# A paired first modulation, a later second modulation and a 32-byte tile in an encoder layer

## The chip, the cores and the metric

The kernel runs on one core of a Trainium2 chip. A core has five engines with queues of their own: TensorE (PE) multiplies matrices, VectorE (DVE) and ScalarE (ACT) work elementwise, GpSimd (POOL) too, and SyncE (SP) mostly issues DMA transfers. They run side by side and wait for each other through semaphores. The metric is the device time of one execution in microseconds (us), the median over runs.

## The reference

One bidirectional encoder layer in float32, 512 tokens of 2048 features. A condition vector c gives six modulation vectors of 2048 each; these are summed over all rows of a 2048 x 12288 matrix, which is 100.7 MB to read.

```
mod = silu(c) @ w_ada + b_ada
sh1, sc1, gt1, sh2, sc2, gt2 = split(mod, 6)
h    = rms_norm(x, g_norm1) * (1 + sc1) + sh1
proj = h @ w_in                        # 8 differential heads, latent q and kv
mix  = concat(diff_attention, latent_attention) @ w_out
x    = x + gt1 * mix
h2   = rms_norm(x, g_norm2) * (1 + sc2) + sh2
x    = x + gt2 * ((silu(h2 @ w_gate) * (h2 @ w_up)) @ w_down)
```

## The kernel before, in words

**Products.** Each float32 operand is split into a rounded high half and the rest (`hi`, `lo`), and a product is three matmuls: hi*hi, hi*lo, lo*hi (`mm3`, lines 241 to 243, in that order on PE). For a weight, `Weights` (lines 60 to 100) loads `raw` by SP (lines 73 and 77, three buffers), ScalarE rounds it to `hi` (line 89), and VectorE or GpSimd subtracts for `lo` (line 97). Which of the two does it stands in the plan of the weights, as "dve", "pool" or "alt" (by turns).

**Modulation sums.** A modulation vector is a sum over the 2048 rows of `w_ada`. A row tile is loaded by SP (line 301), and VectorE multiplies it by a column of silu(c) and adds it to an accumulator `adaacc` (line 305 for the first, line 308 for the rest: scalar_tensor_tensor). A last sum over partitions is a small matmul against ones (`ps_ada`, line 327), and lines 328 to 330 make the columns G and SH from it.

**First stage, to about 180 us.** The 16 blocks of 128 features are taken in the pieces `BLOCKS` = (0,2), (2,2), (4,4), (8,4), (12,4) (start, count). For each piece scale and shift are summed in two accumulators, the normalised x is transposed and modulated (line 378, `hT` split in lines 380 to 382), and the input projection of five heads goes on with that piece (`ps_in`). Partial sums are kept in `raw_in` (line 488). The loads of the modulation use five `araw` buffers; so SP's next load waits for an addition.

**Heads, to about 780 us.** The other heads, the attention, and the first half of the second modulation run interleaved.

**Output projection, about 780 to 930 us.** Four blocks `b` of 512 columns (`ps_o`). Beside them runs a generator `mod2` (line numbers around 1040) that loads and sums the second half of the second modulation, in two groups of four blocks: per group 32 steps that load and sum, six that do nothing, and one that makes the columns. It is taken forward `MOD_PACE[b]` steps per step of the projection. After each block VectorE does the residuals (lines 1053 and 1054, on GpSimd for some), SP stores them to `x1d` (line 1100), ScalarE squares and sums them (line 1102). In the last block a reduction (line 1104) and a reciprocal root on GpSimd (lines 260 and 261) follow each of the four row tiles. Then come the transposes (`ps_xT`, line 1060) and the broadcast of the root (`ps_r`, line 1111).

**Gate and up, about 930 to 1800 us.** First two 256-column pieces in the direct way (`gate_up`, `ps_g` and `ps_u`). Between its products `second_norm` makes the normalised and modulated h2 (lines 1134 to 1136). Then a Strassen-like scheme with seven products of half size (lines 1235 to 1237).

**Down projection, to the end.** `ps_d`, with the activations (`ax`) as stationary operand and the weights' `hi` and `lo` as moving operand.

**Order.** PE's order is the order in which the code issues it. The other four engines get theirs from a scheduler. Each engine works its own queue in order, SP's included.

Of the kernel before, what the change touches and what calls it, by code (L numbers as in the profile page):

```python
# [18 lines left out]
P = 128  # L19
# [117 lines left out]
def weight_plan(a):  # L137
# [61 lines left out]
def hybrid_layer(ctx, tc, a, out):  # L199
# [120 lines left out]

    def ada_columns(sums, k0, nk, G, SH, cg, cbs, cbh):
# [31 lines left out]
    def accs0(dt=F32):  # L353
        return st[1].tile([P, 512], dt, tag="acc", bufs=4, name="adaacc")
# [9 lines left out]
    def modulation_sums(k0, nk):  # L364
        yield from ada_sums(raws0, accs0, 1, 0, k0, nk, 8 // nk, sums1[k0])
# [706 lines left out]
    for b in range(4):  # L1072
# [87 lines left out]
    def gate_up(j, between):  # L1160
# [4 lines left out]
        for k4 in range(4):  # L1165
            for n, pp in (("gate", pg), ("up", pu)):
# [3 lines left out]
                for i in range(4):  # L1170
# [3 lines left out]
                    if G2_done[0] < 4:  # L1174
                        next(mod2, None)
# [177 lines left out]
    gt2 = fd[1].tile([P, D], F32, name="gt2")  # L1353

# [17 lines left out]
    load_acts(1)  # L1372
    W = Wd
# [53 lines left out]
MOD_PACE = (0.3, 2.8, 3.4, 3.2)  # L1427
# [40 lines left out]
```

## Time and profile before

| | |
|---|---|
| median of three runs | 2329.75 us (2326.13 to 2329.98) |
| the profiled execution, its own time | 2330.51 us |
| span in its trace | 2328.1 us |
| PE busy | 2208.3 us (95%) |
| DVE busy | 1634.0 us (70%) |
| ACT busy | 944.7 us (41%) |
| POOL busy | 442.9 us (19%) |
| DMA | 344.98 MB, mean 148 GB/s |

The span runs from the first to the last recorded instruction; the execution's own time is 2.4 us longer. PE is busy nearly all the time, but not in the first eighth and not around 800 to 1000 us. A busy share is an average over stages, so the table of stretches below takes them apart. A row of the timeline gives start, duration, engine, line and operation with the tiles it writes and reads; a bracket at its end holds the idle time before it and what ended it. Rows of PE overlap, since matmuls are pipelined: their pitch, from start to start, is what counts.

### The profile page before, as it was taken

The numbers are of one execution on the slowest core, as the hardware profiler recorded it, in microseconds if no ns is written. First come the engines' busy times: TensorE is split into PE (matmuls) and PEld (weight loads), VectorE is DVE, ScalarE is ACT, GpSimd is POOL, SyncE is SP. The second block draws the span as 40 slices with busy tenths as digits, with TensorE's granted clock in tenths as the row PEclk, the third lists the DMA queues.
The fourth block names the chain that finished last, engine by engine and source line by source line (L and its number), as shares of the span: only waits on it lengthen the run. The fifth ranks groups of instructions, "written<-read, shape, count | busy, mean of one in ns | idle before, by whom it ended". The sixth has DMA issues, their size and how long they took to land.

```text
span 2328.1 us, 35444 instructions
## 1 busy us (share of the span) xinstructions
PE 2208.3 (95%) x13878; PEld 2011.6 (86%) x13878; DVE 1634.0 (70%) x2365; ACT 944.7 (41%) x1569; POOL 442.9 (19%) x492
## 2 busy tenths in 40 slices
PE   2799999999989997999999999999999999999999
PEld 2799989998877785789999999999999877888887
DVE  6987777868898575847777777777777577232543
ACT  4423545566555222434444444444444522121211
POOL 0002433445553622210000000000000221222221
PEclk9899999999999998999999999999999999999999
DMA  9965345422442585243333333333333775232532
GB/s 298 323 216 147 103 138 156 139 88 85 152 157 79 191 286 182 78 131 118 127 115 121 111 126 119 123 112 121 118 127 118 247 263 195 99 128 91 170 129 99
DMA packets 270569, 344.98 MB, mean 148 GB/s; under 512 B 14749, under 2 KB 170886, under 8 KB 270274
## 3 DMA queue, kind: packets, MB, share of 16 engines
q1 hardware_dynamic: 269912, 342.37, 44.9%
q8 instruction: 108, 1.77, 0.3%
q10 hardware_dynamic: 490, 0.36, 0.1%
q14 instruction: 59, 0.48, 0.1%
HBM read 322.71 MB, written 19.96 MB: 147 GB/s over the span
## 4 chain that ended last, share of the span: by engine, by line
PE 57%; DVE 6%; DMA 4%; issue 1%; ACT 1%; SPq 0%; POOL 0%; DVEq 0%; ACTq 0%
PE ps_d L243 6%; PE ps_d L241 6%; PE ps_d L242 6%; PE ps_X L1235 5%; PE ps_X L1236 5%; PE ps_X L1237 5%; PE ps_W L1235 3%; PE ps_W L1236 3%; PE ps_W L1237 3%; DVE adaacc L308 2%; DMA araw<-in_w_ada_dram 2%; PE ps_Y L1235 2%; PE ps_Z L1235 2%; PE ps_Y L1236 2%; PE ps_Z L1236 2%; PE ps_Z L1237 2%
## 5 line engine op out<-in xcount | busy, mean ns | idle before, releaser
L97 POOL TENSOR_TENSOR lo<-raw,hi 128x1024 fp32r<-128x1024 f32 (+1 forms) x75 | 183.6, 2448 | 1403.3 <-ACT hi L89 1384.5
L89 ACT CAST hi<-raw 128x1024 fp32r<-128x1024 f32 (+2 forms) x228 | 221.0, 970 | 508.4 <-PE ps_d L242 286.6
L97 DVE TENSOR_TENSOR lo<-raw,hi 128x768 fp32r<-128x768 f32 (+2 forms) x153 | 168.5, 1101 | 188.5 <-ACT hi L89 184.2
L1235 PE MATMUL ps_X<-comb,wh 128*128 128x256 f32 x960 | 269.7, 281 | 0.0
L1218 ACT CAST wh<-wr 128x1024 fp32r<-128x1024 f32 x160 | 168.6, 1054 | 247.5 <-PE ps_X L1236 69.1
L1236 PE MATMUL ps_X<-comb,wh 128*128 128x256 f32 x960 | 268.8, 280 | 0.0
L1237 PE MATMUL ps_X<-comb,wl 128*128 128x256 f32 x960 | 266.9, 278 | 0.0
L243 PE MATMUL ps_d<-lo,ax 128*128 128x512 f32 x640 | 254.7, 398 | 6.5 <-DVE lo L97 6.5
L241 PE MATMUL ps_d<-hi,ax 128*128 128x512 f32 x640 | 254.3, 397 | 0.0
L242 PE MATMUL ps_d<-hi,ax 128*128 128x512 f32 x640 | 254.1, 397 | 0.0
L1201 DVE TENSOR_TENSOR wl<-wr,wh 128x1024 fp32r<-128x1024 f32 x160 | 195.6, 1222 | 80.2 <-ACT wh L1218 80.0
L241 PE MATMUL ps_in<-hi,hh 128*128 128x384 f32 (+2 forms) x704 | 236.5, 336 | 6.1 <-ACT hi L89 2.7
L243 PE MATMUL ps_in<-lo,hh 128*128 128x384 f32 (+2 forms) x704 | 230.9, 328 | 8.5 <-DVE lo L97 8.5
L242 PE MATMUL ps_in<-hi,hl 128*128 128x384 f32 (+2 forms) x704 | 230.2, 327 | 0.6 <-DVE hl L382 0.6
L1218 ACT CAST wh<-wt 128x1024 fp32r<-128x1024 f32 x120 | 126.2, 1051 | 197.5 <-PE ps_X L1236 120.9
L1201 DVE TENSOR_TENSOR wl<-wt,wh 128x1024 fp32r<-128x1024 f32 x120 | 146.8, 1223 | 81.1 <-ACT wh L1218 81.1
L1236 PEld LDWEIGHTS ps_X<-comb,wh 128*128 128x128 f32 x960 | 180.5, 188 | 0.0
L1237 PEld LDWEIGHTS ps_X<-comb,wl 128*128 128x128 f32 x960 | 180.5, 188 | 0.0
L1235 PE MATMUL ps_W<-comb,wh 128*128 128x256 f32 x640 | 180.0, 281 | 0.4 <-DVE cu L1246 0.4
L1235 PEld LDWEIGHTS ps_X<-comb,wh 128*128 128x128 f32 x960 | 180.2, 188 | 0.0
L1236 PE MATMUL ps_W<-comb,wh 128*128 128x256 f32 x640 | 179.2, 280 | 0.0
L1237 PE MATMUL ps_W<-comb,wl 128*128 128x256 f32 x640 | 177.9, 278 | 0.0
(319 smaller groups left out, 5533.4 us busy)
## 6 DMA issues: line engine op xcount, KB each, us to landing
araw<-in_w_ada_dram SPq DMA_DIRECT2D x96, 512.0 KB
raw<-in_w_down_dram SPq DMA_DIRECT2D x88, 512.0 KB
wr<-in_w_gate_dram SPq DMA_DIRECT2D x40, 1024.0 KB
wr<-in_w_up_dram SPq DMA_DIRECT2D x40, 1024.0 KB
ada<-in_w_ada_dram SPq DMA_DIRECT2D x128, 256.0 KB
raw<-in_w_in_dram SPq DMA_DIRECT2D x128, 192.0 KB
raw<-in_w_out_dram SPq DMA_DIRECT2D x32, 512.0 KB
x<-in_w_ada_dram SPq DMA_DIRECT2D x64, 256.0 KB
```

The costliest lines, as they stand in the source:

```text
L89: nc.scalar.copy(out=hi[:, :n], in_=raw[:, :n])
L97: e.tensor_tensor(out=lo[:, :n], in0=raw[:, :n], in1=hi[:, :n].bitcast(F32), op=ALU.subtract)
L241: pe.matmul(o, ah, bh, start=start, stop=False)
L242: pe.matmul(o, al, bh, start=False, stop=False)
L243: pe.matmul(o, ah, bl, start=False, stop=stop)
L308: dve.scalar_tensor_tensor(out=acc[:, :width], in0=raw[:, i, :width], scalar=c_col[:, q:q + 1], in1=acc[:, :width], op0=ALU.mult, op1=ALU.add)
L1201: dve.tensor_tensor(out=out, in0=x, in1=y, op=ALU.subtract)
L1218: act.copy(out=hi, in_=src)
L1235: pe.matmul(ps[bk], wh[:, k], c[:, 0], start=first and k == 0, stop=False, skip_group_check=True)
L1236: pe.matmul(ps[bk], wh[:, k], c[:, 1], start=False, stop=False, skip_group_check=True)
L1237: pe.matmul(ps[bk], wl[:, k], c[:, 0], start=False, stop=k == 7, skip_group_check=True)
```

## The change

**First modulation.** A new generator `ada_pair` loads scale and shift columns of a row tile into one `araw` tile, laid out row group, scale or shift, column, and sums both in one operation on one accumulator of up to 1024 columns. Two accumulators of 1024 replace four of 512. The two 256-column pieces load two row groups per tile, one DMA each.

**Second modulation.** `MOD_PACE` falls in the last three blocks. 74.4 steps are taken in the projection instead of 100, of 78 that there are. The rest is taken in `second_norm(12)`; the step that stood in `gate_up`'s inner loop is gone. The stores to `x1d` move from SP's queue to ACT's, after each block's residuals. The four reductions and roots of the last block become one of 128x4.

**Weights.** The direct gate and up pieces get "dve" in place of "alt".

**The tile.** A tile of eight floats per partition is allocated in the pool `fd` of the down stage. It is never used. The tiles of that pool, `ax` among them, come to lie 32 bytes lower in each partition.

```
--- before.py
+++ after.py
@@ -180,7 +180,7 @@
     for j in range(STRAIGHT):
         for k4 in range(4):
             for n in ("gate", "up"):
-                plan.append(((n, j, k4), [4, 256], rows(a["w_" + n][0], k4 * 512, 4, j * 256, 256), "alt"))
+                plan.append(((n, j, k4), [4, 256], rows(a["w_" + n][0], k4 * 512, 4, j * 256, 256), "dve"))
     return plan
 
 
@@ -318,6 +318,26 @@
                     yield None
             sums.append(acc)
 
+    def ada_pair(raws, accs, p_scale, p_shift, k0, nk, sums):
+
+        n = nk * P
+        acc = accs()[:, :2 * n].rearrange("p (s n) -> p s n", s=2)
+        nq = 512 // n
+        both = w_ada[:, :, p_shift * D:(p_scale + 1) * D].rearrange("p q (s n) -> p q s n", s=2)
+        for j in range(KC // nq):
+            raw = raws()[:, :2 * nq * n].rearrange("p (q s n) -> p q s n", q=nq, s=2)
+            for i in range(nq):
+                sp.dma_start(out=raw[:, i], in_=both[:, nq * j + i, :, k0 * P:k0 * P + n])
+            for i in range(nq):
+                q = nq * j + i
+                if q == 0:
+                    dve.tensor_scalar(out=acc, in0=raw[:, i], scalar1=c_col[:, 0:1], scalar2=None, op0=ALU.mult)
+                else:
+                    dve.scalar_tensor_tensor(out=acc, in0=raw[:, i], scalar=c_col[:, q:q + 1], in1=acc, op0=ALU.mult,
+                                             op1=ALU.add)
+            yield None
+        sums += [acc[:, 1], acc[:, 0]]
+
     def ada_columns(sums, k0, nk, G, SH, cg, cbs, cbh):
 
         ks = slice(k0, k0 + nk)
@@ -351,7 +371,7 @@
         return st[1].tile([P, 1024], F32, tag="araw", bufs=5, name="araw")
 
     def accs0(dt=F32):
-        return st[1].tile([P, 512], dt, tag="acc", bufs=4, name="adaacc")
+        return st[1].tile([P, 1024], dt, tag="acc", bufs=2, name="adaacc")
 
     ssq1 = st[1].tile([P, NT, 4], F32, name="ssq1")
     rstd1 = st[1].tile([P, NT], F32, name="rstd1")
@@ -362,7 +382,7 @@
     sums1 = {k0: [] for k0, _ in BLOCKS}
 
     def modulation_sums(k0, nk):
-        yield from ada_sums(raws0, accs0, 1, 0, k0, nk, 8 // nk, sums1[k0])
+        yield from ada_pair(raws0, accs0, 1, 0, k0, nk, sums1[k0])
 
     def modulation(k0, nk):
         for b in range(1, 4):
@@ -1097,12 +1117,12 @@
                 transposes(b - 1, spare[0])
         for t in range(NT):
             residual(pss, b, t, gt1, pool if t in OUT_POOL and b < 3 else dve)
-            sp.dma_start(out=x1d[t * P:(t + 1) * P, b * 512:(b + 1) * 512], in_=x1[t][b])
             sq = tmp("sq")
             act.activation(sq, x1[t][b], AF.Square, accum_out=ssq2[:, t, b:b + 1])
-            if b == 3:
-                dve.tensor_reduce(out=rstd2[:, t:t + 1], in_=ssq2[:, t, :], axis=AX.X, op=ALU.add)
-                rsqrt(rstd2[:, t:t + 1], rstd2[:, t:t + 1], 1.0 / D)
+        for t in range(NT):
+            act.dma_start(out=x1d[t * P:(t + 1) * P, b * 512:(b + 1) * 512], in_=x1[t][b])
+    dve.tensor_reduce(out=rstd2, in_=ssq2, axis=AX.X, op=ALU.add)
+    rsqrt(rstd2, rstd2, 1.0 / D)
     while G2_done[0] < 3:
         next(mod2)
     transposes(3, spare[0])
@@ -1128,7 +1148,7 @@
 
     def second_norm(k0):
         while G2_done[0] <= k0 // 4:
-            next(mod2)
+            next(mod2, None)
         for kc in range(k0, k0 + 4):
             xt = x1T[kc]
             dve.scalar_tensor_tensor(out=xt, in0=xt, scalar=G2[:, kc:kc + 1], in1=rB, op0=ALU.mult, op1=ALU.mult)
@@ -1171,8 +1191,6 @@
                     kc = k4 * 4 + i
                     for m in range(2):
                         mm3(pp[m], wh[:, i, tsl(m)], wl[:, i, tsl(m)], h2(kc, 0), h2(kc, 1), kc == 0, kc == KC - 1)
-                    if G2_done[0] < 4:
-                        next(mod2, None)
                 next(between, None)
         sg = wp.tile([P, 1024], F32, tag="raw", bufs=3, name="sg").rearrange("p (m s) -> p m s", m=2)
         for m in range(2):
@@ -1351,6 +1369,7 @@
     fd = open_pool("fd", "right")
     sums = [[fd[1].tile([P, 512], F32, tag="sums", bufs=16, name="sums") for _ in range(4)] for _ in range(NT)]
     gt2 = fd[1].tile([P, D], F32, name="gt2")
+    pads = []
 
     def gate2():
         def raws():
@@ -1370,6 +1389,7 @@
 
     side = gate2()
     load_acts(1)
+    pads.append(fd[1].tile([P, 8], F32, name="pad"))
     W = Wd
     n_parts = len(PARTS)
     j = 0
@@ -1424,7 +1444,7 @@
 DIFF_SIDE = (1, 2, 1, 2, 1, 2, 1, 1)
 MLA_SIDE = (1, 2)
 MOD_EARLY = 8
-MOD_PACE = (0.3, 2.8, 3.4, 3.2)
+MOD_PACE = (0.3, 2.0, 2.5, 2.5)
 MLA_STEPS = "s0 F t0 e F1 t1 s1 v0 F t2 F1 v1 t3 s2 F v2 F1 o0 v3 F o2 o3 s3 o1 F1"
 MLA_FILL = (16.0, 15.7, 16.0, 0.2, 14.1, 19.0, 3.3, 12.8)
```

VectorE's order in the first stage, before: the end of the second piece (numbers at names tell buffers apart; `lo` are low halves of input weights).

```order
L308 SCALAR_TENSOR_TENSOR adaacc_270<-araw_289,c_col_73,adaacc_270 128x256
L308 SCALAR_TENSOR_TENSOR adaacc_295<-araw_296,c_col_73,adaacc_295 128x256
L308 SCALAR_TENSOR_TENSOR adaacc_270<-araw_289,c_col_73,adaacc_270 128x256
L308 SCALAR_TENSOR_TENSOR adaacc_295<-araw_302,c_col_73,adaacc_295 128x256
L308 SCALAR_TENSOR_TENSOR adaacc_270<-araw_289,c_col_73,adaacc_270 128x256
L308 SCALAR_TENSOR_TENSOR adaacc_295<-araw_302,c_col_73,adaacc_295 128x256 x3
L308 SCALAR_TENSOR_TENSOR adaacc_295<-araw_308,c_col_73,adaacc_295 128x256 x2
L97 TENSOR_TENSOR lo_328<-raw_324,hi_327 128x768
L308 SCALAR_TENSOR_TENSOR adaacc_295<-araw_308,c_col_73,adaacc_295 128x256
L97 TENSOR_TENSOR lo_380<-raw_331,hi_379 128x768
L308 SCALAR_TENSOR_TENSOR adaacc_295<-araw_308,c_col_73,adaacc_295 128x256
L305 TENSOR_SCALAR adaacc_358<-araw_359,c_col_73 128x512
```

And now, at the same place:

```order
L336 SCALAR_TENSOR_TENSOR adaacc_261<-araw_277,c_col_73,adaacc_261 128x512 x2
L336 SCALAR_TENSOR_TENSOR adaacc_261<-araw_282,c_col_73,adaacc_261 128x512 x2
L336 SCALAR_TENSOR_TENSOR adaacc_261<-araw_287,c_col_73,adaacc_261 128x512 x2
L336 SCALAR_TENSOR_TENSOR adaacc_261<-araw_292,c_col_73,adaacc_261 128x512 x2
L336 SCALAR_TENSOR_TENSOR adaacc_261<-araw_297,c_col_73,adaacc_261 128x512 x2
L97 TENSOR_TENSOR lo_310<-raw_306,hi_309 128x768
L97 TENSOR_TENSOR lo_360<-raw_313,hi_359 128x768
L334 TENSOR_SCALAR adaacc_340<-araw_341,c_col_73 128x1024
L336 SCALAR_TENSOR_TENSOR adaacc_340<-araw_344,c_col_73,adaacc_340 128x1024
```

One sum of 512 stands where two of 256 stood, and the sums of the second piece are all ahead of the first two low halves, which stood among them.

PE's order around the second group's columns, before (`ps_o` is the output projection):

```order
L241 MATMUL ps_o<-hi,mh 128x512
L242 MATMUL ps_o<-hi,ml 128x512
L243 MATMUL ps_o<-lo,mh 128x512
L327 MATMUL ps_ada<-ones,adaacc 128x1 x8
L241 MATMUL ps_o<-hi,mh 128x512
L242 MATMUL ps_o<-hi,ml 128x512
L243 MATMUL ps_o<-lo,mh 128x512
```

And now (`ps_g` and `ps_u` are gate and up):

```order
L241 MATMUL ps_u<-comb,hi 128x512
L242 MATMUL ps_u<-comb,lo 128x512
L243 MATMUL ps_u<-comb,hi 128x512
L347 MATMUL ps_ada<-ones,adaacc 128x1 x8
L241 MATMUL ps_g<-comb,hi 128x512
L242 MATMUL ps_g<-comb,lo 128x512
L243 MATMUL ps_g<-comb,hi 128x512
```

The columns left the last block of the output projection for the direct gate and up piece, 96 matmuls behind `ps_r`.

VectorE's order at the end of the output projection, before:

```order
L308 SCALAR_TENSOR_TENSOR adaacc<-x_9708,c_col,adaacc 128x512
L308 SCALAR_TENSOR_TENSOR adaacc<-x_9723,c_col,adaacc 128x512
L328 TENSOR_TENSOR G_95<-ps_ada,small 128x4
L330 TENSOR_TENSOR SH_96<-ps_ada,small 128x4
L329 TENSOR_TENSOR G_95<-G_95,small 128x4
L1157 TENSOR_TENSOR shs<-SH_96 128x8
L97 TENSOR_TENSOR lo<-raw,hi 128x1024
L1053 TENSOR_TENSOR tm<-ps_o,gt_8892 128x512
L1054 TENSOR_TENSOR x_8879<-x_8879,tm 128x512
L1053 TENSOR_TENSOR tm<-ps_o,gt_8892 128x512
L1104 TENSOR_REDUCE rstd_8875<-ssq_8874 128x1
L1054 TENSOR_TENSOR x_8883<-x_8883,tm 128x512
```

And now:

```order
L1073 TENSOR_TENSOR tm<-ps_o,gt_8823 128x512
L308 SCALAR_TENSOR_TENSOR adaacc<-x_9815,c_col,adaacc 128x512
L1074 TENSOR_TENSOR x_8810<-x_8810,tm 128x512
L308 SCALAR_TENSOR_TENSOR adaacc<-x_9818,c_col,adaacc 128x512
L1073 TENSOR_TENSOR tm<-ps_o,gt_8823 128x512
L1074 TENSOR_TENSOR x_8814<-x_8814,tm 128x512
L1073 TENSOR_TENSOR tm<-ps_o,gt_8823 128x512
L97 TENSOR_TENSOR lo<-raw,hi 128x1024
L1074 TENSOR_TENSOR x_8818<-x_8818,tm 128x512
L1073 TENSOR_TENSOR tm<-ps_o,gt_8823 128x512
L1074 TENSOR_TENSOR x_8822<-x_8822,tm 128x512
L1124 TENSOR_REDUCE rstd_8806<-ssq_8805 128x4
```

The last sums stand beside the first residual of the last block instead of ahead of the columns' G and SH, and one reduction of 128x4 follows the last residual.

## Rows read from the trace of the kernel before

**Rows 1.** The table of stretches: per engine busy us (instructions), then granted clock, DMA share, rate.
```profile
41.00:120.00 79.00, 60.73 (x319) 57.20 (x320) 77.56 (x137) 35.34 (x59) 0.00 (x0) 0.91 0.99 322
...
802.00:900.00 98.00, 81.42 (x376) 66.73 (x374) 80.92 (x96) 26.77 (x46) 26.56 (x12) 0.94 0.83 274
...
930.00:1030.00 100.00, 95.60 (x417) 78.00 (x418) 68.56 (x105) 42.69 (x63) 19.11 (x7) 0.97 0.31 99
1030.00:1850.00 820.00, 819.61 (x6826) 813.19 (x6825) 617.65 (x641) 364.47 (x452) 8.20 (x5) 1.00 0.38 126
```

**Rows 2.** What TensorE waited for, 0 to 320 us: total us, times, longest us.
```profile
PE ps_ada L327 <- DVE adaacc L308: 36.1, 4, 17.4
PE ps_in L243 <- DVE lo L97: 8.5, 4, 5.6
```

**Rows 3.** The table of stretches, two windows of ten microseconds.
```profile
50.00:60.00 10.00, 8.10 (x49) 7.67 (x49) 9.96 (x21) 4.18 (x8) 0.00 (x0) 1.00 1.05 354
100.00:110.00 10.00, 4.46 (x24) 3.81 (x23) 10.00 (x18) 4.75 (x8) 0.00 (x0) 0.86 0.90 296
```

**Rows 4.** What the SyncE queue waited for, 0 to 180 us.
```profile
SPq L301 <- DVE adaacc L308: 58.9, 44, 4.0
```

**Rows 5.** Lines by form, VectorE, 0 to 180 us: busy us, mean ns, idle before.
```profile
L308 DVE SCALAR_TENSOR_TENSOR adaacc<-araw,c_col,adaacc 128x512 f32<-128x512 f32 x90 | 66.4, 744 | 0.2
L308 DVE SCALAR_TENSOR_TENSOR adaacc<-araw,c_col,adaacc 128x256 f32<-128x256 f32 x60 | 28.0, 482 | 7.8 <-DMA araw<-in_w_ada_dram 6.6
```

**Rows 6.** TensorE's timeline in the first stage: start us, us, instruction.
```profile
113.18 0.52 PE L241 MATMUL ps_in<-hi,hh 128*128 128x384 f32 x1
...
117.76 0.33 PE L241 MATMUL ps_in<-hi,hh 128*128 128x384 f32 x1
...
119.00 0.33 PE L242 MATMUL ps_in<-hi,hl 128*128 128x384 f32 x1
```

**Rows 7.** TensorE's timeline in the output projection; idle before in brackets.
```profile
899.63 1.87 PE L327 MATMUL ps_ada<-ones,adaacc 128*128 128x1 f32 x8 [10.95 <-DVE adaacc L308]
...
901.93 0.63 PE L242 MATMUL ps_o<-hi,ml 128*128 128x512 f32 x1
...
905.77 0.49 PE L242 MATMUL ps_o<-hi,ml 128*128 128x512 f32 x1
```

**Rows 8.** VectorE's timeline in the output projection.
```profile
880.67 0.75 DVE L308 SCALAR_TENSOR_TENSOR adaacc<-x,c_col,adaacc 128x512 f32<-128x512 f32 x1 [2.65 <-DMA x<-in_w_ada_dram]
881.33 1.22 DVE L97 TENSOR_TENSOR lo<-raw,hi 128x1024 fp32r<-128x1024 f32 x1
...
887.52 2.85 DVE L308 SCALAR_TENSOR_TENSOR adaacc<-x,c_col,adaacc 128x512 f32<-128x512 f32 x1
...
922.50 0.69 DVE L1054 TENSOR_TENSOR x<-x,tm 128x512 f32<-128x512 f32 x1
...
924.12 2.62 DVE L1054 TENSOR_TENSOR x<-x,tm 128x512 f32<-128x512 f32 x1
```

**Rows 9.** GpSimd's timeline in the output projection.
```profile
886.86 2.96 POOL L97 TENSOR_TENSOR lo<-raw,hi 128x1024 fp32r<-128x1024 f32 x1 [12.70 <-ACT hi L89]
...
923.86 2.34 POOL L97 TENSOR_TENSOR lo<-raw,hi 128x1024 fp32r<-128x1024 f32 x1
```

**Rows 10.** What the SyncE queue waited for, 800 to 930 us.
```profile
SPq L1100 <- DVE x L1054: 25.1, 12, 4.8
```

**Rows 11.** TensorE's timeline, output projection at full clock.
```profile
831.86 0.39 PE L243 MATMUL ps_o<-lo,mh 128*128 128x512 f32 x1
...
837.98 0.39 PE L243 MATMUL ps_o<-lo,mh 128*128 128x512 f32 x1
```

**Rows 12.** TensorE's timeline, down projection.
```profile
1999.61 0.40 PE L243 MATMUL ps_d<-lo,ax 128*128 128x512 f32 x1
...
2011.51 0.40 PE L243 MATMUL ps_d<-lo,ax 128*128 128x512 f32 x1
```

**Rows 13.** Lines by form, TensorE, 1850 to 2328 us.
```profile
L241 PE MATMUL ps_d<-hi,ax 128*128 128x512 f32 x640 | 254.3, 397 | 0.0
```

More of the change, by code (lines that the diff above doesn't have):

```diff
@@ L182, in weight_plan @@
             for n in ("gate", "up"):
-                plan.append(((n, j, k4), [4, 256], rows(a["w_" + n][0], k4 * 512, 4, j * 256, 256), "alt"))
+                plan.append(((n, j, k4), [4, 256], rows(a["w_" + n][0], k4 * 512, 4, j * 256, 256), "dve"))
     return plan
@@ L319, in ada_sums, with ada_pair @@
             sums.append(acc)
+    def ada_pair(raws, accs, p_scale, p_shift, k0, nk, sums):
+        n = nk * P
+        acc = accs()[:, :2 * n].rearrange("p (s n) -> p s n", s=2)
+        nq = 512 // n
+        both = w_ada[:, :, p_shift * D:(p_scale + 1) * D].rearrange("p q (s n) -> p q s n", s=2)
+        for j in range(KC // nq):
+            raw = raws()[:, :2 * nq * n].rearrange("p (q s n) -> p q s n", q=nq, s=2)
+            for i in range(nq):
+                sp.dma_start(out=raw[:, i], in_=both[:, nq * j + i, :, k0 * P:k0 * P + n])
+            for i in range(nq):
+                q = nq * j + i
+                if q == 0:
+                    dve.tensor_scalar(out=acc, in0=raw[:, i], scalar1=c_col[:, 0:1], scalar2=None, op0=ALU.mult)
+                else:
+                    dve.scalar_tensor_tensor(out=acc, in0=raw[:, i], scalar=c_col[:, q:q + 1], in1=acc, op0=ALU.mult,
+                                             op1=ALU.add)
+            yield None
+        sums += [acc[:, 1], acc[:, 0]]
     def ada_columns(sums, k0, nk, G, SH, cg, cbs, cbh):
@@ L353, in accs0 @@
     def accs0(dt=F32):
-        return st[1].tile([P, 512], dt, tag="acc", bufs=4, name="adaacc")
+        return st[1].tile([P, 1024], dt, tag="acc", bufs=2, name="adaacc")
     ssq1 = st[1].tile([P, NT, 4], F32, name="ssq1")
@@ L364, in modulation_sums @@
     def modulation_sums(k0, nk):
-        yield from ada_sums(raws0, accs0, 1, 0, k0, nk, 8 // nk, sums1[k0])
+        yield from ada_pair(raws0, accs0, 1, 0, k0, nk, sums1[k0])
     def modulation(k0, nk):
@@ L1099, in hybrid_layer @@
             residual(pss, b, t, gt1, pool if t in OUT_POOL and b < 3 else dve)
-            sp.dma_start(out=x1d[t * P:(t + 1) * P, b * 512:(b + 1) * 512], in_=x1[t][b])
             sq = tmp("sq")
             act.activation(sq, x1[t][b], AF.Square, accum_out=ssq2[:, t, b:b + 1])
-            if b == 3:
-                dve.tensor_reduce(out=rstd2[:, t:t + 1], in_=ssq2[:, t, :], axis=AX.X, op=ALU.add)
-                rsqrt(rstd2[:, t:t + 1], rstd2[:, t:t + 1], 1.0 / D)
+        for t in range(NT):
+            act.dma_start(out=x1d[t * P:(t + 1) * P, b * 512:(b + 1) * 512], in_=x1[t][b])
+    dve.tensor_reduce(out=rstd2, in_=ssq2, axis=AX.X, op=ALU.add)
+    rsqrt(rstd2, rstd2, 1.0 / D)
     while G2_done[0] < 3:
@@ L1130, in second_norm @@
         while G2_done[0] <= k0 // 4:
-            next(mod2)
+            next(mod2, None)
         for kc in range(k0, k0 + 4):
@@ L1173, in gate_up @@
                         mm3(pp[m], wh[:, i, tsl(m)], wl[:, i, tsl(m)], h2(kc, 0), h2(kc, 1), kc == 0, kc == KC - 1)
-                    if G2_done[0] < 4:
-                        next(mod2, None)
                 next(between, None)
@@ L1353, in hybrid_layer @@
     gt2 = fd[1].tile([P, D], F32, name="gt2")
+    pads = []
     def gate2():
@@ L1372, in hybrid_layer @@
     load_acts(1)
+    pads.append(fd[1].tile([P, 8], F32, name="pad"))
     W = Wd
@@ L1426 @@
 MOD_EARLY = 8
-MOD_PACE = (0.3, 2.8, 3.4, 3.2)
+MOD_PACE = (0.3, 2.0, 2.5, 2.5)
 MLA_STEPS = "s0 F t0 e F1 t1 s1 v0 F t2 F1 v1 t3 s2 F v2 F1 o0 v3 F o2 o3 s3 o1 F1"
```

## The prediction

> **What bounds the kernel now.** I read first the table of stretches [rows 1]. From 1030 to 1850 us TensorE works 819.61 of 820 us: there nothing but the matmuls' own pitch can give time. TensorE lacks work in three places: 18.3 of the 79 us from 41 to 120, 16.6 of the 98 us from 802 to 900, and 4.4 of the 100 us from 930 to 1030. So the change is worth what it does in those places, and what it does to the pitch of the last stage.
>
> The list of what TensorE waited for says what ends its gaps in the first stage [rows 2]: 36.1 us in four waits for the summed modulation columns, and 8.5 us for low halves of weights that VectorE makes. One 17.4 us wait is the start, before any product is possible, and is not to be had. In 41 to 120 us VectorE is busy 77.56 of 79 us and the DMA share is 0.99 at 322 GB/s [rows 1]: two resources are full at once. The two ten-microsecond windows [rows 3] tell them apart a little: 354 GB/s were moved where all went well, and 296 GB/s (share 0.90) where VectorE was busy 10.00 of 10 us and TensorE only 4.46. The SyncE queue waits 58.9 us, 44 times, for an addition to free a buffer before it issues the next load [rows 4]. VectorE therefore comes first, and DMA stands close behind.
>
> In the output projection the one large wait is 10.95 us, before the second group's columns at 899.63 [rows 7]. VectorE's rows show why: the additions wait for their DMA for the last time at 880.67, and from there they stand in line among residuals and low halves [rows 8].
>
> For the last stage I read the distance between starts of matmuls. In the output projection 9 rounds of the three products take 6.12 us, 0.2267 us each matmul [rows 11]; in the down projection 17 rounds take 11.90 us, 0.2333 us each [rows 12], for the same 128x512 shape.
>
> **The change part by part.** The sum is made against the profiled execution's own 2330.51 us (span 2328.1); that is 0.8 us over the median shown, so the result compares with the median unchanged.
>
> First modulation. Removed: 60 sums 256 wide and 90 sums 512 wide, at 482 and 744 ns [rows 5], 94.4 us of durations. Added: 30 sums 512 wide and 45 sums 1024 wide. A 1024-wide sum is in no row; from 256 to 512 it grows by 262 ns, so two such steps more give 1268 ns (between 744, if width cost nothing, and 1488, twice the 512). That is 22.3 + 57.1 = 79.4 us, 15.0 less. Rows that follow each other overlap a little (the 0.75 us from 880.67 reach past 881.33, where the next begins [rows 8]), so 80 rows fewer save somewhat less: 10 to 15 us of VectorE. The bytes stay the same and so do the runs of the DMAs. If VectorE gives way, DMA bounds: 79 us at 322 GB/s are 25.4 MB, at 354 GB/s 71.9 us, 7.1 us less. To this comes part of the time at the lower clock: from 113.18 to 117.76 fifteen matmuls take 4.58 us, against 0.177 us each just after, so 1.9 us lost [rows 6]; the granted clock of 41 to 120 is 0.91 [rows 1], and this stretch stands right behind a gap of 5.6 us [rows 2]. Half of the loss may go with the gap. Against it, each block's last addition is longer by 0.5 us (three blocks on the path). I take -8. Bounds: -18, all of TensorE's lack of work there; +2, if DMA is full anyway and only the longer last addition and one longer tile (524 KB at 322 GB/s, 1.63 us) count.
>
> Spread-out second modulation. The sums per column block fall, so that some stand later; but the columns are asked for later too: the first group's by 48 matmuls (11 us at 0.2267), the second group's after the residuals, behind 96 gate and up matmuls (22 us). VectorE's order has the last sum between the first residuals of the last block, as the listing of its end shows, so the columns are ready some 20 us ahead of need. The 10.95 us go [rows 7], and with them the slow matmuls right behind: 901.93 to 905.77 is 9 matmuls in 3.84 us, 0.427 each, where 0.2267 is full speed: 1.8 us [rows 7]. The tail: a POOL low half at 923.86 holds the residual at 924.12 for 2.62 us where the one at 922.50 took 0.69 [rows 8, 9]; that low half is one of gate or up and moves to VectorE, -1.9. What is late next are the four residuals with their squares, one reduction and one rsqrt; the last square came last before, so I count the merging as nothing. Sum -14.7. I add 2 for one low half held as at 887.52 (2.85 us where such sums take 0.75 [rows 8, 9]) by the POOL halves that stay. I take -13; bounds -17 and -3 (a new wait of nearly the size of the old one).
>
> The x1d stores: SyncE waited 25.1 us in 12 waits for residuals before it could issue them [rows 10], with loads behind. On ScalarE's queue each store comes behind a square that has waited for the same residual, so it adds no wait; sixteen issues stand on an engine busy 26.77 of 98 us [rows 1]. Counted in the -13, since it only lets loads go sooner.
>
> Gate and up low halves: eight leave POOL for VectorE at 1.22 us [rows 8], 9.8 us more on an engine busy 68.56 of 100 [rows 1]. Against it no POOL half holds VectorE by about 2 us. TensorE lacks 4.4 us there, the most to be won; half of the 9.8 us, if they come at the head of the stage, is the most that I let it lose. I take -1, bounds -4.4 and +5.
>
> The 32-byte tile. It moves the stationary operand of the down products (`ax`) by 32 bytes. As built, `ax` begins 32 bytes past a multiple of 64 before and the moving weights `hi`, `lo` at a multiple of 64; now both begin at the same place modulo 64. In the output projection, where both operands stand alike, the pitch is 0.2267; in the down projection, where they stand unlike, it is 0.2333. The lines by form have 640 such products for each of three lines [rows 13]: 1920 x 0.0066 = 12.6 us. I take -12; bounds -13 and 0, since the two stages differ in more than this offset.
>
> The Trainium skill, "SBUF — State Buffer", section "SBUF: two separate sides", says that among engines only the port pair shared by VectorE and GpSimd causes contention, and that TensorE never waits on anyone. No run here shows why 0.2333 and 0.2267 differ. By the rows the step is worth 12 us, by that rule nothing; the first rival carries it.
>
> The sum: 2330.5 - 8 - 13 - 1 - 12 = 2296.5 us. All bounds together: 2278 (-18 -17 -4.4 -13) and 2334.5 (+2 -3 +5).
>
> **The rivals.** First, the 32-byte tile does nothing: the slower pitch belongs to something else in the down stage, such as its weight traffic. For it: nothing in the trace names the operands' place as the cause; against it: the pitch is steady over 17 rounds, not a burst. 2296.5 + 12 = 2308.5 us.
>
> Second, the first stage stays as it is because DMA at share 0.99 sets it [rows 1]. For it: that number; against it: 354 GB/s in one window and the 44 waits for buffers [rows 3, 4]. 2296.5 + 8 = 2304.5 us.
>
> Third, the spread modulation only moves its wait: the second group's columns are late in the gate stage or the weights behind the loads are, so that it gains 3 instead of 13. 2306.5 us. Against it: about 20 us of slack.
>
> Fourth, slower: in the first stage an addition now needs its whole tile, scale and shift, and VectorE takes its work in order. If it stands waiting for the tile at the head of that line, the low halves behind it, for which TensorE waits [rows 2], wait as well. A tile takes 1.63 us at 322 GB/s, and there are 48 wide ones; the other parts bring 26 us, so from 16 such waits on the kernel is slower. With 24 of them: 2330.5 - 26 + 39 = 2343.5 us. Against it: SyncE waits for VectorE, not the other way round, 58.9 us long [rows 4].
>
> That nothing of it works, or that small losses eat the gains, leaves 2326 to 2335 us.
>
> **How the numbers follow.** Chances: forecast 0.46, first rival 0.20, second 0.14, third 0.11, fourth 0.06, nothing 0.03. The range is 2278 to 2319 us: its low end is all bounds together, its high end takes in the first three rivals and the first two together (2316.5); the fourth and the last stay out. A measurement of this kernel tells 0.2%, 4.7 us, from no change. All cases up to the third are more than that faster: 0.91; the last is the same, 0.03; the fourth is slower, 0.06.
>
> **What would show it.** In the changed kernel's table of stretches VectorE's busy time up to the first full stretch should fall by 10 to 15 us, the 1024-wide sum should take about 1.27 us, and the DMA rate from 41 to 110 should rise above 335 GB/s; TensorE's full work should begin some 8 us sooner. The wait of 10.95 us should be missing, with none over 3 us between the output projection and the gate stage, and no POOL low half between 920 and 1000 us. The down matmuls should start 0.227 us apart; 0.2333 again would prove the first rival. A first stage of unchanged length with share 0.99 proves the second; waits of VectorE's sums for DMA, over 25 us in sum and with TensorE waiting for low halves behind them, the fourth.

## The result and the profile after

The changed kernel takes 2295.07 us (median of four runs, 2292.43 to 2296.81), the kernel before 2327.94 us with one more run than shown above (2325.54 to 2329.98): ratio 0.9848, 95% interval 0.9834 to 0.9863. The forecast was 2296.5 us in 2278 to 2319. The sum came out, in part by luck: the terms for the first modulation and for gate and up missed in opposite directions, and so did two steps inside the term for the second modulation, as the runs below show.

The table of stretches of the changed kernel (columns as in [rows 1]), its stages being up to 22 us earlier than before:

```profile
0.00:41.00 41.00, 3.98 (x17) 3.45 (x17) 16.62 (x31) 17.73 (x41) 1.41 (x6) 1.00 0.91 290
41.00:120.00 79.00, 64.48 (x325) 60.80 (x326) 73.60 (x93) 35.46 (x59) 0.00 (x0) 0.89 0.99 320
120.00:180.00 60.00, 60.00 (x359) 57.96 (x358) 47.45 (x75) 18.36 (x25) 0.00 (x0) 1.00 0.70 211
775.00:890.00 115.00, 110.57 (x515) 90.81 (x514) 78.84 (x89) 33.05 (x55) 46.27 (x25) 1.00 0.76 261
890.00:920.00 30.00, 21.96 (x83) 16.58 (x82) 25.14 (x35) 11.61 (x21) 3.62 (x3) 0.73 0.57 192
920.00:1020.00 100.00, 100.00 (x502) 85.20 (x502) 71.73 (x114) 42.51 (x63) 0.00 (x0) 0.99 0.34 111
```

In 41 to 120 us TensorE does 64.48 us of work where it did 60.73 [rows 1], and VectorE 73.60 where it did 77.56; the DMA share is 0.99 as before and the rate 320 GB/s (324 from 41 to 110 us), not above 335. TensorE's last wait ahead of its full work ends at 111.71 us, 1.0 us sooner than before and not 8. In 775 to 890 TensorE is busy 110.57 of 115 us: the gap of 10.95 us [rows 7] is gone. But 890 to 920 is poor: 21.96 of 30, granted clock 0.73. From 920 to 1020 there is no gap at all.

Starts of products in the two profiled executions say how much each stage gave:

| product (TensorE) | before, us | after, us | gained since the row above |
|---|---|---|---|
| first `ps_in` | 41.18 | 41.15 | 0.0 |
| 401st `ps_in` | 145.53 | 144.51 | 1.0 |
| first `ps_o` | 583.78 | 581.49 | 1.3 |
| first `ps_xT` of the third block | 906.33 | 884.24 | 19.8 |
| first `ps_g` | 931.22 | 914.90 | -5.8 |
| first `ps_X` | 1026.16 | 1006.96 | 2.9 |
| first `ps_d` | 1818.07 | 1792.76 | 6.1 |
| last `ps_d` | 2323.01 | 2285.59 | 12.1 |

The sum is 37.4 us, a little more than the medians' 32.9. The 6.1 us of the Strassen stage can't be put down to an edit. Its code is the same in both kernels, and so are the places of its operands as built; among the thirteen profiles of kernels in which these did not change (before, after and eleven of the experiments), the stretch from the first `ps_X` to the 2801st took between 759.3 and 766.8 us, whatever had been edited elsewhere. Before's profile has 765.5, after's 759.6.

What TensorE waited for between 760 and 1060 us in the changed kernel (total us, times, longest us):

```profile
PE ps_xT L1080 <- DVE x L1074: 5.2, 4, 2.4
PE ps_o L243 <- POOL lo L97: 3.5, 2, 3.1
PE ps_g L241 <- ACT comb L1155: 1.6, 1, 1.6
PE ps_r L1131 <- POOL rstd L261: 1.3, 1, 1.3
```

No wait is over 3.1 us now (that one lies in the output projection, ahead of 812 us), but `ps_xT` has four that come with the last residuals and `ps_r` one for the merged root: a new tail. TensorE's timeline shows it, from the last product of the output projection to the first of gate and up:

```profile
900.42 0.39 PE L243 MATMUL ps_o<-lo,mh 128*128 128x512 f32 x1
903.20 0.63 PE L1080 MATMUL ps_xT<-ident,x 128*128 128x128 f32 x4 [2.39 <-DVE x L1074]
905.16 1.12 PE L1080 MATMUL ps_xT<-ident,x 128*128 128x128 f32 x4 [1.34 <-DVE x L1074]
907.50 1.12 PE L1080 MATMUL ps_xT<-ident,x 128*128 128x128 f32 x4 [1.22 <-DVE x L1074]
908.82 1.11 PE L1080 MATMUL ps_xT<-ident,x 128*128 128x128 f32 x4 [0.21 <-DVE x L1074]
911.23 2.08 PE L1131 MATMUL ps_r<-ident,rstd 128*128 128x128 f32 x8 [1.29 <-POOL rstd L261]
914.90 0.79 PE L241 MATMUL ps_g<-comb,hi 128*128 128x512 f32 x1 [1.59 <-ACT comb L1155]
```

From 900.42 to 914.90 are 14.5 us. Before it was 9.7:

```profile
921.50 0.39 PE L243 MATMUL ps_o<-lo,mh 128*128 128x512 f32 x1
...
931.22 0.50 PE L241 MATMUL ps_g<-comb,hi 128*128 128x512 f32 x1 [1.59 <-ACT comb L1135]
```

VectorE's rows of the changed kernel's timeline show what stands there:

```profile
887.96 11.43 DVE L308 SCALAR_TENSOR_TENSOR adaacc<-x,c_col,adaacc 128x512 f32<-128x512 f32 x12 [0.36 <-DMA x<-in_w_ada_dram]
899.31 1.22 DVE L97 TENSOR_TENSOR lo<-raw,hi 128x1024 fp32r<-128x1024 f32 x1
900.45 0.74 DVE L308 SCALAR_TENSOR_TENSOR adaacc<-x,c_col,adaacc 128x512 f32<-128x512 f32 x1
...
901.71 0.74 DVE L308 SCALAR_TENSOR_TENSOR adaacc<-x,c_col,adaacc 128x512 f32<-128x512 f32 x1
902.37 0.68 DVE L1074 TENSOR_TENSOR x<-x,tm 128x512 f32<-128x512 f32 x1
902.97 0.74 DVE L308 SCALAR_TENSOR_TENSOR adaacc<-x,c_col,adaacc 128x512 f32<-128x512 f32 x1
...
909.62 0.17 DVE L1124 TENSOR_REDUCE rstd<-ssq 128x4 f32<-128x16 f32 x1 [0.85 <-ACT sq L1121]
```

Twelve sums stand in one piece behind a DMA, a low half follows, and three more sums lie ahead of and among the first residuals: the first residual is done at 903.05, 2.6 us after TensorE's last product has started.

The sums of the first stage, in the lines by form (columns as in [rows 5]):

```profile
L336 DVE SCALAR_TENSOR_TENSOR adaacc<-araw,c_col,adaacc 128x1024 f32<-128x1024 f32 x45 | 57.5, 1278 | 1.1 <-DMA araw<-in_w_ada_dram 0.9
...
L336 DVE SCALAR_TENSOR_TENSOR adaacc<-araw,c_col,adaacc 128x512 f32<-128x512 f32 x30 | 22.5, 751 | 12.7 <-DMA araw<-in_w_ada_dram 11.9
```

And the down products, in the same view of TensorE:

```profile
L242 PE MATMUL ps_d<-hi,ax 128*128 128x512 f32 x640 | 249.6, 390 | 0.0
...
L242 PE MATMUL ps_d<-hi,act 128*128 128x512 f32 x54 | 21.4, 396 | 0.0
```

1278 ns for the new sum (estimated 1268). The products on `ax` fall from 397 ns [rows 13] to 390, the few on `act`, whose tile was not moved, stay at 396. And the pitch itself, from the timeline, between rows of one line as in [rows 12]:

```profile
1999.99 0.39 PE L243 MATMUL ps_d<-lo,ax 128*128 128x512 f32 x1
...
2011.55 0.39 PE L243 MATMUL ps_d<-lo,ax 128*128 128x512 f32 x1
```

17 rounds in 11.56 us, 0.2267 us each matmul: the pitch of the output projection [rows 11].

### The profile page after: what moved, and what is told of

It is laid out like the page before. It is cut to its first block, busy times and chain, and to the rows that moved or that the text cites. A ratio compares the mean times of both kernels' runs of the same rounds, so it can differ in the third digit from the quotient of the medians.

```text
span 2290.6 us, 35353 instructions
## 1 busy us (share of the span) xinstructions
PE 2183.1 (95%) x13878; PEld 1999.4 (87%) x13878; DVE 1625.7 (71%) x2290; ACT 945.3 (41%) x1569; POOL 418.2 (18%) x478
## 4 chain that ended last, share of the span: by engine, by line
PE 60%; DVE 8%; DMA 5%; issue 2%; ACT 1%; SPq 0%; POOL 0%; DVEq 0%; ACTq 0%; POOLq 0%
PE ps_d L243 6%; PE ps_d L242 6%; PE ps_d L241 6%; PE ps_X L1253 5%; PE ps_X L1254 5%; PE ps_X L1255 5%; PE ps_W L1253 3%; PE ps_W L1255 3%; PE ps_W L1254 3%; DVE adaacc L308 3%; DMA araw<-in_w_ada_dram 2%; DMA x<-in_w_ada_dram 2%; PE ps_Z L1253 2%; PE ps_Y L1253 2%; PE ps_Y L1255 2%
## 5 line engine op out<-in xcount | busy, mean ns | idle before, releaser
L97 POOL TENSOR_TENSOR lo<-raw,hi 128x1024 fp32r<-128x1024 f32 (+1 forms) x67 | 161.4, 2410 | 1386.0 <-DMA raw<-in_w_down_dram 879.9
L97 DVE TENSOR_TENSOR lo<-raw,hi 128x1024 fp32r<-128x1024 f32 (+2 forms) x161 | 178.7, 1110 | 168.3 <-ACT hi L89 164.3
L242 PE MATMUL ps_d<-hi,ax 128*128 128x512 f32 x640 | 249.6, 390 | 0.0
L241 PE MATMUL ps_d<-hi,ax 128*128 128x512 f32 x640 | 249.6, 390 | 0.0
```

Source lines behind the costliest of these rows:

```text
L97: e.tensor_tensor(out=lo[:, :n], in0=raw[:, :n], in1=hi[:, :n].bitcast(F32), op=ALU.subtract)
L241: pe.matmul(o, ah, bh, start=start, stop=False)
L242: pe.matmul(o, al, bh, start=False, stop=False)
```

## The experiments

**One part at a time.** Four kernels are the kernel before with one edit of the change.

The tile alone, `e1_pad32`:

```
     load_acts(1)
+    pads.append(fd[1].tile([P, 8], F32, name="pad"))
```

> The kernel before with the 32-byte tile alone. Theory (the place of the stationary operand modulo 64 bytes sets the pitch): down matmuls 0.2267 us apart instead of 0.2333, the last stage and the whole kernel 12 to 13 us shorter, everything ahead of it as before. Rival (the tile does nothing and the last stage gained in another way, by earlier weights): pitch 0.233, the whole within 3 us of before.

Measured: 2318.96 us, ratio 0.9955 (0.9936 to 0.9974). The lines by form of its last stage:

```profile
L241 PE MATMUL ps_d<-hi,ax 128*128 128x512 f32 x640 | 249.1, 389 | 0.0
...
L241 PE MATMUL ps_d<-hi,act 128*128 128x512 f32 x64 | 25.3, 395 | 0.0
```

389 ns, starts 0.227 us apart, and a gain of 12.4 us from the first to the last `ps_d`, against before. The rival falls.

Twice the size, `e2_pad64`: `[P, 16]` in place of `[P, 8]`, so that the tiles go down by 64 bytes.

> The kernel before with a tile of 64 bytes in the same place: the tiles move by 64 bytes, so their place modulo 64 is that of before. Theory of the place modulo 64: pitch 0.233, time as before within 3 us. Rival (any move of the tiles, or their place in a larger unit, does it): pitch 0.227, 12 us less.

Measured: 2328.60 us, ratio 1.0001 (0.9982 to 1.0020). The same line of its last stage:

```profile
L241 PE MATMUL ps_d<-hi,ax 128*128 128x512 f32 x640 | 253.4, 396 | 0.0
```

396 ns, starts 0.234 us apart: nothing gained. A move by 64 bytes does nothing where one by 32 does. Other distances were not run, so "modulo 64" stands for these two.

The other operand moved, `e9_weights32`: the kernel before, with the 32 bytes ahead of the weights of the Strassen and the down stage.

```
         fw.append(open_pool("fw"))
+        wpads.append(fw[0][1].tile([P, 8], F32, name="wpad"))
```

> The kernel before with a 32-byte tile ahead of the weights of the Strassen and down stages, instead of among the activations: the moving weights of the down products go up by 32 bytes and ax stays. Theory (what counts is that both operands begin at the same place modulo 64 bytes): down matmuls 0.2267 us apart, 12 us less in the last stage, as with the activations moved. Rival (ax at a multiple of 64 is what counts): 0.233, no gain. For the Strassen products, whose operands then stand alike too, the theory wants less than their 0.116 to 0.117 us; a rule that holds for 512 columns alone wants no change.

Measured: 2337.73 us, ratio 1.0033 (1.0020 to 1.0046), so 0.33% slower. The lines by form of its down stage:

```profile
L241 PE MATMUL ps_d<-hi,ax 128*128 128x512 f32 x640 | 249.1, 389 | 0.0
...
L241 PE MATMUL ps_d<-hi,act 128*128 128x512 f32 x46 | 17.9, 389 | 0.0
```

The same view of its Strassen stage:

```profile
L1236 PE MATMUL ps_X<-comb,wh 128*128 128x256 f32 x944 | 267.2, 283 | 0.0
```

And of the kernel before's, for comparison:

```profile
L1235 PE MATMUL ps_X<-comb,wh 128*128 128x256 f32 x946 | 265.7, 281 | 0.0
```

In the down stage all products now take 389 ns, those on `act` too (395 or 396 elsewhere): that both operands begin alike modulo 64 is what counts, and not that `ax` begins at a multiple of 64. From the first to the last `ps_d` it gains 11.9 us, as the theory said. The 256-column products of the Strassen stage go the other way, 283 ns for each of the three lines against 281, 280 and 278: alike they start 0.120 us apart, and steadily so (2757 of 2760 distances between `ps_X` products are 120 ns); unlike they start 0.1166 to 0.1178 us apart on average in the other thirteen profiles. The stage is 14 us longer than in before's profile (779.8 us to the 2801st `ps_X`, against 765.5, and 759.3 to 766.8 in all the others), which is more than the down stage gains. My expectation for these products was wrong: the rule holds for 512 columns and turns round at 256. The 256-column products of the input projection, whose operands begin alike in the kernel before as built, stand 0.120 us apart too (the median in its profile).

The paired first modulation alone, `e3_pair` (`ada_pair` and the accumulators of 1024 columns):

> The kernel before with the paired first modulation alone. Theory (DMA sets the first stage, so VectorE's 10 us are cover): the 200th product of the input projection starts 0 to 2 us sooner than before, the whole 0 to 3 us shorter. Rival (the prediction's term, VectorE sets it and gives 8 us): 6 to 10 us shorter, lost again in the whole change to something else.

Measured: 2326.24 us, ratio 0.9980 (0.9961 to 0.9999), some 4.7 us of 2329.75 with an interval from 0.2 to 9. The median lies between theory and rival, and the interval reaches into both. The stage varies from one execution to the next. So I compare all profiles with the first stage as it was (before and five experiments) to those with the pair (after and five): the 401st `ps_in` starts at 145.5, 149.2, 147.2, 151.8, 153.2, 153.4 us without, mean 150.1, and at 144.5, 143.9, 145.5, 143.6, 146.4, 143.8 with, mean 144.6. The pair is worth 5.4 us in its stage. Before's profile was the quickest of its six, which is why the table above shows 1.0.

What varies is mostly TensorE's work at a lower granted clock: between the first and the 401st `ps_in` it is busy for 86.3 to 93.5 us, at a mean granted clock of 0.94 down to 0.88, in the six without the pair. Its time without work there is steady, 17.9 to 18.7 us without and 13.2 to 14.4 with, 18.2 and 14.0 on average. In the rows of the kernel before and of the changed kernel it is the stretch less the first busy time:

```profile
41.18:145.53 104.35, 86.26 (x477) 82.62 (x477) 101.30 (x177) 43.23 (x69) 0.00 (x0) 0.93 0.98 316
...
41.15:144.51 103.36, 88.99 (x476) 85.19 (x477) 95.74 (x124) 43.38 (x69) 0.00 (x0) 0.92 0.98 313
```

Half of the bytes, `e6_pair_half` (of the changed kernel) and `e7_before_half` (of before): every second tile is loaded, each summed twice, all sums remain.

```
+            if j % 2 == 0:
+                raw = raws()[:, :2 * nq * n].rearrange("p (q s n) -> p q s n", q=nq, s=2)
+            for i in range(nq if j % 2 == 0 else 0):
                 sp.dma_start(out=raw[:, i], in_=both[:, nq * j + i, :, k0 * P:k0 * P + n])
```

These are the lines of `e6_pair_half` without those they replace; `e7_before_half` does the same in `ada_sum`.

> The changed kernel, where the first modulation loads every second tile only and sums each tile twice (the modulation is then of other numbers): half the bytes of that load, all of the sums. Theory (DMA sets the first stage in the changed kernel): the 200th product of the input projection starts 8 us or more sooner than in the changed kernel. Rival (VectorE or TensorE's own waits set it): within 3 us.

> The kernel before with the same load left out: every second tile of the first modulation is loaded, and each is summed twice. Theory (two resources full at once, VectorE close behind DMA): it gains less than the changed kernel does from the same cut, and the difference between the two cut kernels is the 8 to 10 us that VectorE saves. Rival (VectorE alone sets the stage before): no gain here, within 2 us.

Measured: 2291.30 us (ratio 0.9832, 0.9817 to 0.9847) and 2321.53 us (0.9961, 0.9948 to 0.9974). The 401st `ps_in` starts at 136.5 and at 140.7 us: 8.1 and 9.4 sooner than the means above. Of this, 2.7 and 3.0 us come ahead of the first product, which starts at 38.7 and 38.5 us where the means are 41.5 and 41.6. In the time, `e6_pair_half` is only 3.8 us under the changed kernel, with intervals that overlap. The 200th product, which the expectation named, starts 5.0 us sooner than in the changed kernel, which lies between its two cases. Both parts of the theory for `e7_before_half` missed: its cut gains no less than the changed kernel's, and the two cut kernels lie 4.2 us apart at the 401st product instead of 8 to 10. Its rival, no gain, falls too. The table of stretches of the first:

```profile
41.00:120.00 79.00, 67.31 (x374) 65.54 (x374) 75.88 (x96) 34.13 (x57) 0.00 (x0) 0.96 0.66 204
```

And of the second:

```profile
41.00:120.00 79.00, 65.45 (x348) 63.97 (x349) 75.94 (x132) 32.67 (x55) 0.00 (x0) 0.91 0.62 187
```

With DMA at 0.66 and 0.62, TensorE still lacks 11.7 and 13.6 us there. So half of this load costs the stage 8 to 9 us in either kernel, start included, and the pair gives 4.2 us with the load halved (one pair of profiles), 5.4 with all of it: neither resource alone sets the stage, and that DMA hides the pair's gain is not seen. That VectorE alone set it before falls as well.

The pace alone, `e4_pace` (`MOD_PACE` and the two edits of `next(mod2)`):

> The kernel before with the new pace of the second modulation alone (stores, roots, weights and the rest as before). Theory (the 10.95 us wait and the slow matmuls behind it go by the pace alone): start of the gate stage 10 to 14 us sooner. Rival (the stores on ScalarE's queue and the weights are needed for it): less than 7 us sooner.

Measured: 2317.24 us, ratio 0.9946 (0.9928 to 0.9964), 12.6 us of 2329.75. From the first `ps_xT` to that of the third block it gains 18.0 us against before, and from there to the first `ps_g` it loses 7.5: the gap goes by the pace alone, and the new tail comes with it. Together the gate stage starts 10.5 us sooner, counted from the first `ps_xT`, which is within the theory; in the profile's own time it starts 3.5 us sooner only, since the first stage took 6.3 us longer in that execution.

The low halves alone, `e5_dve` (`"alt"` to `"dve"`):

> The kernel before with the eight low halves of gate and up on VectorE alone. Theory (GpSimd's low half held the last residual for 2.62 us, and its slow halves held TensorE a little in the gate stage): from the last product of the output projection to the first Strassen product 3 to 5 us less, the whole 2 to 5 us less. Rival (9.8 us more on VectorE delay TensorE): that stretch 0 to 5 us longer.

Measured: 2323.51 us, ratio 0.9968 (0.9957 to 0.9980), 7.5 us of 2329.75. The table of stretches from the first `ps_g` to the first `ps_X`, of the kernel before:

```profile
931.22:1026.16 94.94, 91.76 (x384) 74.16 (x385) 64.02 (x100) 39.91 (x60) 19.11 (x7) 0.96 0.32 100
```

And of this kernel:

```profile
938.88:1029.07 90.19, 90.19 (x384) 73.92 (x385) 65.97 (x107) 39.90 (x60) 0.00 (x0) 0.97 0.33 106
```

94.94 us become 90.19. The 3.2 us in which TensorE was idle are gone (91.76 of 94.94, now 90.19 of 90.19), and its work itself is 1.6 us shorter at a granted clock of 0.97 in place of 0.96. VectorE has 65.97 of 90 us to do: it holds the eight low halves easily. Another 1.2 us go in the tail (from the first of the last block's transposes to the first `ps_g`: 9.5 to 8.3). Together 6.0 us from the last product of the output projection to the first Strassen product, more than the theory's 3 to 5; the rival falls.

**The rest of the part.** `e10_stores_back` is the changed kernel with the stores on SyncE's queue and the four reductions and roots again.

> The changed kernel with the x1d stores back on SyncE's queue and the reduction and root per row tile again. Theory (that part is worth nothing, the others sum to the whole): within 3 us of the changed kernel, some 2295 us; the tail from the last product of the output projection to the gate stage 1 us shorter than its 14.5, as the one root of four columns is longer and later. Rival (the stores held up the loads): 4 us or more slower than the changed kernel.

Measured: 2297.44 us, ratio 0.9864 (0.9845 to 0.9883), which overlaps the changed kernel's 0.9834 to 0.9863: nothing that can be told. Its tail is 15.5 us, not shorter. Yet `ps_r` follows the transposes without a wait, so the wait for the merged root is not by itself what makes the tail long. Its gate stage takes 89.7 us where the changed kernel's takes 92.1; TensorE's granted clock there is 1.00 against 0.97.

The four single ratios multiply to 0.9980 x 0.9946 x 0.9968 x 0.9955 = 0.9850; the whole is 0.9848. That one part hides another is not seen; the four intervals together leave some 0.3% (8 us) open. The stores and the root are worth nothing that these runs can tell.

**Can the tail be mended?** `e8_tail` takes the sums earlier, `e11_late` later, `e12_mix` is `e10_stores_back` with a pace between. Each changes one line of the changed kernel (or of `e10_stores_back`):

```
-MOD_PACE = (0.3, 2.0, 2.5, 2.5)
+MOD_PACE = (0.3, 2.0, 3.2, 1.8)      # e8_tail
+MOD_PACE = (0.3, 2.0, 2.5, 1.2)      # e11_late
+MOD_PACE = (0.3, 2.0, 2.5, 1.8)      # e12_mix
```

> The changed kernel with the same number of steps of the second modulation, more of them in the third block and fewer in the last (3.2 and 1.8 per step in place of 2.5 and 2.5), so that the last sums come before the last residuals. Theory (three sums among the last residuals hold them back): from the last product of the output projection to the first of the gate stage 14.5 us become 11 to 13, the whole 1 to 4 us less than the changed kernel. Rival (the merged root after all squares makes the tail): still 14 to 15 us.

> The changed kernel with 1.2 steps instead of 2.5 in the last block of the output projection: eight sums of the second modulation now stand behind the first norms of the gate stage, none among the last residuals. Theory (the sums among the residuals and those just ahead hold back the tail): 14.5 us of tail become 10 to 11; the whole 2 to 4 us less, if the columns are in time. Rival (the columns come late and TensorE waits for them in the gate stage): a wait for them of over 3 us there, time as the changed kernel or more.

> The changed kernel with the stores on SyncE's queue and the root per row tile again, and 1.8 steps in the last block instead of 2.5, so that three sums stand in the gate stage and one or two among the last residuals. Theory (tail and columns can be balanced): tail 11 to 13 us, gate stage 90 to 92 us, the whole 2 to 4 us less than the changed kernel's 1.5% under before. Rival (what leaves the tail comes back as a wait for the columns, as with 1.2 steps): gate stage 94 us or more, the whole as the changed kernel within 2 us.

Measured: ratios 0.9847 (0.9825 to 0.9870), 0.9867 (0.9847 to 0.9886) and 0.9843 (0.9821 to 0.9866); medians 2296.52, 2298.75 and 2294.14 us. VectorE's rows in `e8_tail` at the end of the output projection:

```profile
897.84 2.41 DVE L308 SCALAR_TENSOR_TENSOR adaacc<-x,c_col,adaacc 128x512 f32<-128x512 f32 x3 [0.98 <-DMA x<-in_w_ada_dram]
901.55 0.75 DVE L308 SCALAR_TENSOR_TENSOR adaacc<-x,c_col,adaacc 128x512 f32<-128x512 f32 x1 [1.30 <-DMA x<-in_w_ada_dram]
...
903.92 1.22 DVE L97 TENSOR_TENSOR lo<-raw,hi 128x1024 fp32r<-128x1024 f32 x1
```

The last sums stand ahead of the residuals there, and wait for their DMA: the loads are not sooner because the steps are, so the tail stays at 14.6 us and the theory falls. In `e11_late`, with the merged root and no sums there, the transposes follow the last product at once:

```profile
902.69 0.39 PE L243 MATMUL ps_o<-lo,mh 128*128 128x512 f32 x1
902.92 0.60 PE L1080 MATMUL ps_xT<-ident,x 128*128 128x128 f32 x4
...
913.85 0.79 PE L241 MATMUL ps_g<-comb,hi 128*128 128x512 f32 x1 [1.59 <-ACT comb L1155]
```

The tail shrinks to 11.2 us, so the sums and not the merged root make most of it. What it gains is lost, as the rival said: the gate stage is 97.5 us, with this wait in it:

```profile
PE ps_ada L347 <- DVE adaacc L308: 3.3, 1, 3.3
```

`e12_mix` has 13.8 us of tail, over the theory's 11 to 13, and 91.4 of gate stage; it does not differ from the changed kernel in the time. None of the three is better than it by what the runs can tell.

## Why the sum came out, point by point

**The 32-byte tile: right, in size and reason.** Forecast 12, measured 12.1 in the changed kernel's last stage, 12.4 alone, and 0.45% (0.26 to 0.64) of the time. The first rival falls: `e1_pad32` and `e2_pad64` differ by 32 bytes of unused memory and 0.4% of the time. The Trainium skill ("SBUF — State Buffer", section "SBUF: two separate sides") says that TensorE never waits on anyone. Read as the prediction read it, that the place of an operand is then worth nothing, it does not agree with these runs: 0.2333 us against 0.2267. Why the pitch depends on the places is not shown here. My reason was too wide in one point: operands that begin alike are quicker at 512 columns and slower at 256.

**The spread-out modulation: right in sum, by two steps that were wrong in opposite directions.** Forecast 13 (10.95 and 1.8 for the gap and its slow matmuls, 1.9 for the tail, 2 against). The gap went whole, and gave more than the 12.75 forecast. The stretch from the first `ps_xT` to the third block's, before and now:

```profile
816.17:906.33 90.16, 77.19 (x354) 63.84 (x353) 67.26 (x87) 22.25 (x38) 15.96 (x6) 0.92 0.80 269
...
812.15:884.24 72.09, 71.58 (x337) 59.06 (x336) 53.57 (x67) 21.89 (x36) 14.90 (x6) 1.00 0.76 265
```

Of 18.1 us, 12.5 are time without work. Another 2.8 are the last columns' own matmuls, which moved to the gate stage, and the last 2.8 are work that ran at a granted clock of 0.92 and now at 1.00: I had counted only the slow matmuls right behind the gap. The step that failed is "What is late next are the four residuals with their squares": I had the order before me, with two of the three sums among the last residuals, and costed them at nothing. The tail grew by 4.8 us where I had it shrink by 1.9. `e11_late`, without sums there, gets 3.3 of the 4.8 back. What the remaining 1.4 over before are is not shown; in that tail stand a low half of 1.22 us between the residuals and a wait of 1.29 for the merged root, which I had counted as nothing. The 1.9 us belong to the low halves' part: `e5_dve` alone gains 1.2 in its tail. The third rival, that the wait moves into the gate stage, holds in `e11_late` with 3.3 us, where the steps are still fewer, and not in the changed kernel.

**Gate and up: right in sign, mis-sized.** Forecast 1, bounds 4.4 gained and 5 lost; `e5_dve` measured 4.75 in the stage and 0.32% (0.20 to 0.43), some 7.5 us, in the time. I took the most that could be had as TensorE's 4.4 us without work, and set against it up to half of 9.8 us on VectorE, a cost that did not come. The 1.6 us of work at a lower granted clock were left out; the tail stood in the part above.

**First modulation: mis-sized the other way.** Forecast 8, measured 5.4 in the stage and 4.7 (0.2 to 9) in the time, which by itself does not exclude 8. VectorE's saving came. The sums alone, in the table of stretches from 41 to 120 us, before and now:

```profile
41.00:120.00 79.00, 56.19 (x91) 0.91 0.99 322
...
41.00:120.00 79.00, 49.91 (x46) 0.89 0.99 320
```

To 180 us they take 97.0 us before and 83.2 now, 13.8 less, within the forecast 10 to 15. All of VectorE's busy time falls by 9.9 only (from 147.6 to 137.7), since 3.9 us of other work has come forward. But 3.9 of the 13.8 fall before 41 us, where the first product starts at the same moment, and 3.6 after 120, where TensorE had all it could do before as now:

```profile
120.00:180.00 60.00, 59.96 (x354) 57.25 (x353) 49.29 (x91) 17.86 (x24) 0.00 (x0) 1.00 0.66 202
```

Only 6.3 lie in between. The step that failed is "If VectorE gives way, DMA bounds": 7.1 of the 8 us came from a rate of 354 GB/s, and the rate stayed at 320. I also read the waits too large: of the 36.1 us for the columns [rows 2] all but 3.7 stand ahead of the first product. What TensorE waited for from 41 to 120 us, that row before and the largest one now:

```profile
PE ps_ada L327 <- DVE adaacc L308: 3.7, 2, 2.5
...
PE ps_in L243 <- DVE lo L97: 10.8, 4, 5.1
```

The waits for the columns are gone, those for low halves have grown from 8.5 us [rows 2], and the one of 5.6, with which half of the slow matmuls were to go, is still there with 5.1. The working has a slip too, which does not move the forecast: its 94.4 us are busy time, from which the overlap is already out, and not durations (60 x 482 and 90 x 744 ns are 95.9 us). The second rival (DMA sets the stage) has the share 0.99 right and the conclusion wrong; by the sign that I gave for it, a stage of unchanged length, the one pair of profiles with its 1.0 us would nearly have passed as proof, and only the other ten and `e3_pair` say otherwise. The fourth (VectorE waits for whole tiles) did not show: of VectorE's waits for those loads 11.9 us stand ahead of the 512-wide sums of the first two pieces, and 0.9 ahead of the 1024-wide ones on which it rested.

## What to carry to other kernels

A gain on one engine is to be laid out over the stage's windows before it is counted, by the rows that change and not by the engine's busy time, into which other work moves: of 13.8 us here 6.3 lay where TensorE waited, and some 5 came back. When a wait is moved, read the rows now queued in its new place as costs, even if they are a handful. And where two stages of one shape have steadily different pitches, compare early where their operands begin.

## What was not expected of the hardware

The start of a matmul's operands modulo 64 bytes moves its pitch: at 512 columns 0.2267 us alike and 0.2333 unlike (`e1_pad32`, `e2_pad64`, `e9_weights32`), at 256 columns a steady 0.120 alike (`e9_weights32`) and 0.1166 to 0.1178 unlike (all others). And the same instructions with the same operand places in the Strassen stage took 759.3 to 766.8 us in thirteen kernels, 1% with TensorE busy without a break; a single profile pair can put 6 us on a stage that no edit has touched. What sets it stays open.
